# Where the tiles of a two-layer decoder trunk begin in SBUF: every dynamic tile at a multiple of 256 bytes, one weight form split in two halves

## The chip, the cores and the metric

One core of one Trainium2 chip runs the whole program. The metric is the device time of one execution in microseconds (us), the median of three runs. TensorE (PE) multiplies; VectorE (DVE), ScalarE (ACT) and GpSimd (POOL) prepare its operands and collect its results; SyncE (SP) issues the loads from HBM, and GpSimd issues some transfers too. SBUF is the memory from which TensorE reads, PSUM the one to which it writes. A place in SBUF is given here as a byte offset inside a partition; all 128 partitions hold the same layout.

## The reference

A sequence of 512 tokens of width 1024 goes through two layers. Each layer is a half-step SwiGLU, a mixer, and another half-step SwiGLU:

```
for l in range(2):
    x = x + 0.5 * swiglu(rms_norm(x, ffn_norm[l, 0]), w_gate[l, 0], w_up[l, 0], w_down[l, 0])
    h = rms_norm(x, mix_norm[l])
    m = hybrid_mixer(h, ...) if l == 0 else sparse_attention(h, ...)
    x = x + m
    x = x + 0.5 * swiglu(rms_norm(x, ffn_norm[l, 1]), w_gate[l, 1], w_up[l, 1], w_down[l, 1])

def swiglu(h, w_gate, w_up, w_down):
    return (silu(h @ w_gate) * (h @ w_up)) @ w_down
```

The SwiGLU's inner width is 2816. The hybrid mixer of layer 0 projects 1024 to 5656 columns, runs a Mamba-2 scan and an mLSTM on them, and projects 2048 columns back to 1024. The mixer of layer 1 is attention over 128 keys that an indexer picks for each query. All of it is in float32.

## The kernel before, in words

**Products.** A float32 weight block is cut by `made` and `both` into two float32r parts, a high and a low one: ScalarE copies the high part (line 361), VectorE subtracts to get the low part (line 363). Where `summed` is set, ScalarE writes the negated copy (line 391), a transfer from GpSimd's queue adds the block to it (line 392), and ScalarE writes the high part (line 393). The two parts together are called a form. The activations are cut the same way. `mm3` (lines 241 to 243) then multiplies with three matmuls: high by high, high by low, low by high. Each matmul has its own weight load, so TensorE alternates weight loads (128 columns) and matmuls.

**Seven instead of eight.** `seven` and `product_seven` compute a 2x2 block product with seven block products, from sums of the blocks. `unit_seven` is one unit of 256 of the 2816 inner columns, for gate and up together: seven block products, each with two halves of 128 columns (`s` = 0, 1), four row blocks (`q`) and three matmuls of 256 columns, so 7 x 2 x 4 x 3 = 168 matmuls. A SwiGLU has eleven units in groups of 4, 4 and 3; its first two units are done plainly by `unit` with matmuls of 512 columns, and nine by `unit_seven`. After each group `down` runs the output projection of that group as two more products of the seven-product kind, with as many row blocks as the group has units. That makes 9 x 168 + 4 x 7 x 2 x 3 x (4 + 4 + 3) / 2 = 1512 + 924 = 2436 matmuls of 256 columns in each of the four SwiGLUs. The hybrid mixer's input projection has six more such products with the weights as stationary operand, and four with the two operands exchanged (`tok=True`).

**Slots of the forms.** `ring("any")` deals out slots in turn. Slots 0 to 3 are parts of one static tile, `form`; the last one, slot 4, is a dynamic tile made by `one_form`. The hybrid mixer uses slots 0 to 3 only. The order of the tensor work is that of the program within a stream; the planner (`Plan`) orders the other engines around it by its costs and due times, and neither knows of addresses.

**Places.** The static tiles lie in this order: `raw` from byte 1152, which is (10 x 1024 + 512 + 16) x 4 = 43,072 bytes long; `form` from byte 44,224, 4 x 8192 bytes long; `ft` from byte 76,992, 16,384 bytes long. So the slots 0 to 3 begin at byte 192 past a multiple of 256 (192 mod 256), and the space for dynamic tiles begins at byte 93,376, which is 192 mod 256 too. An allocator places the dynamic tiles (activation forms `xf` and `hid`, the plain activations `xgn`, `one_form` and all the scratch) in that space, by their lifetimes. Before the change most of them sit at 0 mod 256, some at 192 and some at 224, the last because `hv` is 257 numbers wide. `one_form` sits at 0 mod 256. The dynamic space is nearly full: it is packed up to byte 228,160 of 228,192.

Of the kernel before, what the change touches and what calls it, by code (L numbers as in the profile page):

```python
# [11 lines left out]
F32R = mybir.dt.float32r  # L12
# [4 lines left out]
P = 128  # L17
# [26 lines left out]
PERIODS = [(p, _pieces(p, 4)) for p in (2 * math.pi * 512, 2 * math.pi)]  # L44
NRAW, NFORM = 4, 5
H = T // 2
# [160 lines left out]


class LazyFeat(Feat):
    def __getitem__(self, k):  # L210
# [3 lines left out]
class Trunk:  # L214
# [17 lines left out]

    def one_form(self):


        return Later(lambda: self.part.tile([P, 2, 1024], F32R, name="form", tag="form"))

# [136 lines left out]

    def made(self, block, summed=False):

        i, raw = block
        _, n, w = raw.shape
        j, f = self.ring("any")
        slot = f  # L380
        f = Later(lambda: slot[:, :, 0 : n * w].rearrange("p i (n w) -> p i n w", w=w))
        self.both(lambda: f, [("f", j, 0)], [("f", j, 1)], raw, [("raw", i)], summed)
        return j, f
# [105 lines left out]
    def seven(self, raws, xf, late, kept, evac):  # L489
# [6 lines left out]
        nq = len(xf)  # L496
        i, two = "sum", self.box
        t2 = i, two[:, 0 : nq * 256].rearrange("p (n w) -> p n w", w=256)

        def mul(ps, block, form, start, summed=False, f=None, ss=(0, 1)):  # L500
            j, f = made = f or self.made(block, summed)
            ps, psk = ps
            for s in ss:
                col = slice(s * P, (s + 1) * P)
                for q in range(nq):
                    self.times(
                        ps, psk, s, (j, lambda q=q, col=col: (f[:, 0, q, col], f[:, 1, q, col])),
                        lambda q=q: xf[q][0](form), xf[q][1](form), start and q == 0, q == nq - 1, not start, H, 0.355,
                    )
            return made  # L510
# [251 lines left out]
    def product_seven(self, raws, xf, kept, evac, tok, summed, scale):  # L762
# [3 lines left out]
        c11, c12, c21, c22 = evac  # L766
        two = "sum", self.box

        def mul(ps, block, form, start, ss=(0, 1), f=None):
            j, f = made = f or self.made(block, form in summed)  # L770
            bank, psk = ps
            for s in ss:
                col = slice(s * P, (s + 1) * P)
                for q in range(4):
                    if tok:
                        l = lambda q=q, col=col: [x[:, col] for x in xf[q][0](form)]
                        r = lambda q=q: (f[:, 0, q], f[:, 1, q])
                    else:
                        l = lambda q=q, col=col: (f[:, 0, q, col], f[:, 1, q, col])
                        r = lambda q=q: xf[q][0](form)  # L780
                    self.t(0.355, lambda l=l, r=r, s=s, q=q: self.mm3(
                        bank()[:, s * H : (s + 1) * H], l(), r(), start and s == 0 and q == 0, q == 3, True,
                    ), [("f", j, 0), ("f", j, 1)] + xf[q][1](form), [psk])
            return made
# [119 lines left out]
    def hybrid(self, nxt):  # L904
# [42 lines left out]
        def rows(c0, tag, width, func=None):  # L947

            half = [self.spot(tag, (NB, 2, width), 2) for _ in range(2)]
            at = lambda b, h: half[h // 2][0]()[:, b, h % 2]  # L950
            key = lambda b, h: (*half[h // 2][1], b, h)
# [101 lines left out]
    def gated(self, xs, hid, free):  # L1053

        nc, par = self.nc, self.par
        for grp in range(2):
# [13 lines left out]
            ps, psk = self.bank("hc")  # L1070
            col, ck = self.spot("hcol", (2, NB), 2)
            ms, rc = (lambda i=i, col=col: col()[:, i] for i in range(2))
# [281 lines left out]
    def mlstm(self, q, k, vt, og, g, hid):  # L1354
# [4 lines left out]
        (vx, vk), (ox, ok) = vt, og  # L1359
        st, stk = self.spot("cst", (4, 257), 1)  # L1360
        x4 = lambda t: t().rearrange("p (a b) -> p a b", a=4)
# [32 lines left out]
        for c in range(NB):  # L1394
            e, ek, qs, qsk, kt = ahead
            if c < NB - 1:
                ahead = weights(c + 1)
            ev, evk = self.spot("gev", (4, 4), 2)
            den, ss, rd, r = (lambda i=i, ev=ev: ev()[:, i] for i in range(4))
            part = lambda i: (*evk, i)  # L1400
            for h in range(4):
                ps, psk = self.bank("hc")

                def go(ps=ps, h=h, c=c, e=e, qs=qs):
                    nc.tensor.matmul(ps()[:, 0:257], e()[:, h], vx(c, h), start=True, stop=(c == 0))
                    if c:
                        nc.tensor.matmul(ps()[:, 0:257], qs()[:, h], st()[:, h], start=False, stop=True)

# [6 lines left out]
            if c < NB - 1:  # L1415
                for h in range(4):
# [4 lines left out]
                    if c:  # L1421
                        self.v(300, lambda ps=ps, h=h, c=c: nc.vector.scalar_tensor_tensor(
                            st()[:, h], st()[:, h], aa()[:, c, h : h + 1], ps()[:, 0:257], op0=ALU.mult, op1=ALU.add), [psk, sk, aak], [sk])
                    else:
                        self.v(257, lambda ps=ps, h=h: nc.vector.tensor_copy(st()[:, h], ps()[:, 0:257]), [psk], [sk])
            v4 = lambda issue, rd_, wr: self.v(4, issue, rd_, wr)
# [113 lines left out]
    def attention(self, nxt):  # L1540
# [4 lines left out]
        xg, xgk, rcol = self.xg, self.xgk, self.rcol  # L1545
        plan.stream = "filler"


# [329 lines left out]
        out(1, range(4, KC), True)  # L1878
        plan.stream = plan.floor = None

    def topk(self, sc, sk, m8, n):
# [14 lines left out]
    def run(self, stages=STAGES):  # L1896
        tc = self.tc
        with ExitStack() as ctx:
# [15 lines left out]
            self.rrow, raw = raw[:, 0:T], raw[:, T + 16 :].rearrange("p (i n) -> p i n", n=1024)  # L1914
            form = self.res.tile([P, NFORM - 1, 2, 1024], F32R, name="form")
            self.places = self.res.tile([P, 2, 8, H], F32, name="ft")
# [51 lines left out]
```

## Time and profile before

| | |
|---|---|
| median of three runs | 1998.28 us (1989.86 to 2009.0) |
| the profiled execution | 1994.66 us |
| its span, first to last instruction | 1992.6 us |
| mean granted TensorE clock | 0.994 |
| TensorE busy | 1945.2 us, 14594 matmuls |
| VectorE busy | 1633.1 us |
| ScalarE busy | 1266.3 us |

How to read the lines that follow: a row of the timeline is "start us, duration us, engine, line, operation, output<-inputs, shape, count", with idle time before it in brackets and what ended it. Matmuls overlap in the pipeline, so the duration of one (0.28 us for 256 columns) says little; the distance from one start to the next is what a matmul costs, and the prediction works with that distance. A row of the windows gives, for a stretch of time, its length and for each engine the busy time and the count of instructions, then the granted clock (PEclk) and the DMA share. A row of the groups gives line, engine, operation, operands, shape, count, then busy us, mean ns, and idle time before.

### The profile page before, as it was taken

Reading aid. Unit: us, or ns where it says so; the run is one execution under the profiler, and the core shown is the slowest. Engines: PE = TensorE matmul, PEld = TensorE weight load, DVE = VectorE, ACT = ScalarE, POOL = GpSimd, SP = SyncE. Lnnn points to the kernel's source line nnn. Section 1 sums busy time; section 2 is a strip of 40 time slices with the busy share of each in tenths; the row PEclk is TensorE's granted clock in tenths of the full one; section 3 lists DMA queues with packets and bytes.
Section 4 is the critical chain, followed back from the end, with each engine's and each line's share of the span. In section 5 each row is a group of like instructions: output and inputs, shape, how many; then the busy total and the mean of one; then the engine's idle time right before and its main releaser. Section 6 shows DMA issues by size and latency. Waiting matters only on the chain.

```text
span 1992.6 us, 36277 instructions
## 1 busy us (share of the span) xinstructions
PE 1945.2 (98%) x14594; PEld 1802.2 (90%) x14594; DVE 1633.1 (82%) x2383; ACT 1266.3 (64%) x1906; POOL 321.7 (16%) x401
## 2 busy tenths in 40 slices
PE   8999999999998999999999999999999999999998
PEld 6999999799887888999998899999956587999998
DVE  6888888987889558988888998978778747989886
ACT  6666656567768545657566575756756844757564
POOL 1000001222234110010002010000423521101010
PEclk9999999999999999999999999999999999999999
DMA  8566666467768342666665366666744302666564
GB/s 222 138 157 154 171 157 161 130 164 186 206 174 236 94 135 64 168 155 172 153 155 141 105 154 166 172 156 154 191 106 96 75 14 72 159 160 166 152 172 114
DMA packets 226609, 292.87 MB, mean 147 GB/s; under 512 B 15037, under 2 KB 196489, under 8 KB 225929
## 3 DMA queue, kind: packets, MB, share of 16 engines
q1 hardware_dynamic: 200728, 199.30, 32.4%
q0 software_dynamic: 25632, 91.24, 24.4%
q8 instruction: 114, 1.87, 0.4%
q14 instruction: 55, 0.44, 0.1%
q10 hardware_dynamic: 80, 0.02, 0.0%
HBM read 192.96 MB, written 6.33 MB: 100 GB/s over the span
## 4 chain that ended last, share of the span: by engine, by line
PE 77%; DMA 8%; DVE 8%; issue 5%; ACT 1%; POOL 1%; SPq 0%; POOLq 0%; ACTq 0%; DVEq 0%
PE pA L242 9%; PE pA L243 9%; PE pA L241 9%; PE pD L241 4%; PE pD L242 4%; PE pD L243 4%; DMA form<-raw 3%; PE hm L241 3%; PE hm L242 3%; PE hm L243 3%; PE pB L241 2%; PE pB L242 2%; PE pB L243 2%; DVE form L363 2%; DMA raw<-in_hy_w_in 2%
## 5 line engine op out<-in xcount | busy, mean ns | idle before, releaser
L363 DVE TENSOR_TENSOR form<-raw,form 128x1024 fp32r<-128x1024 f32 (+2 forms) x382 | 455.9, 1198 | 98.8 <-ACT form L361 97.1
L361 ACT ACTIVATE form<-raw 128x1024 fp32r<-128x1024 f32 (+2 forms) x382 | 392.3, 1030 | 219.1 <-DVE raw L356 148.2
L392 POOL DMA_DIRECT2D form<-raw x172 | 150.2, 874 | 1322.7 <-ACT form L391 1271.4
L356 DVE TENSOR_TENSOR raw<-raw 128x1024 f32<-128x1024 f32 (+2 forms) x281 | 334.8, 1196 | 21.6 <-DMA raw<-in_ffn_w_down 11.6
L241 PE MATMUL pA<-xf,form 128*128 128x256 f32 x1152 | 321.8, 279 | 0.0
L243 PE MATMUL pA<-xf,form 128*128 128x256 f32 x1152 | 321.4, 279 | 0.0
L242 PE MATMUL pA<-xf,form 128*128 128x256 f32 x1152 | 321.2, 279 | 0.0
L391 ACT ACTIVATE form<-raw 128x1024 fp32r<-128x1024 f32 (+1 forms) x172 | 178.4, 1038 | 159.3 <-PE pD L243 73.6
L241 PEld LDWEIGHTS pA<-xf,form 128*128 128x128 f32 x1152 | 217.3, 189 | 0.4
L243 PEld LDWEIGHTS pA<-xf,form 128*128 128x128 f32 x1152 | 217.3, 189 | 0.1
L242 PEld LDWEIGHTS pA<-xf,form 128*128 128x128 f32 x1152 | 217.2, 189 | 0.2
L242 PE MATMUL pA<-hid,form 128*128 128x256 f32 x704 | 198.4, 282 | 2.8 <-DVE hid L363 2.7
L243 PE MATMUL pA<-hid,form 128*128 128x256 f32 x704 | 197.3, 280 | 3.4 <-DVE form L363 3.4
L241 PE MATMUL pA<-hid,form 128*128 128x256 f32 x704 | 198.3, 282 | 0.9 <-DVE ft L356 0.3
L393 ACT ACTIVATE form<-raw 128x1024 fp32r<-128x1024 f32 (+1 forms) x172 | 176.6, 1028 | 0.0
L241 PE MATMUL pD<-xf,form 128*128 128x256 f32 x576 | 160.5, 279 | 0.0
L243 PE MATMUL pD<-xf,form 128*128 128x256 f32 x576 | 160.5, 279 | 0.0
L242 PE MATMUL pD<-xf,form 128*128 128x256 f32 x576 | 160.4, 279 | 0.0
L356 DVE TENSOR_TENSOR ft<-ft 128x256 f32<-128x256 f32 (+2 forms) x296 | 151.5, 544 | 3.4
L242 PEld LDWEIGHTS pA<-hid,form 128*128 128x128 f32 x704 | 132.8, 189 | 4.7 <-DVE hid L363 4.6
L243 PEld LDWEIGHTS pA<-hid,form 128*128 128x128 f32 x704 | 132.8, 189 | 3.6 <-DVE form L363 3.6
L241 PEld LDWEIGHTS pA<-hid,form 128*128 128x128 f32 x704 | 132.7, 188 | 2.1 <-DVE ft L356 0.9
(452 smaller groups left out, 5342.2 us busy)
## 6 DMA issues: line engine op xcount, KB each, us to landing
form<-raw POOLq DMA_DIRECT2D x156, 512.0 KB, 5.6
raw<-in_ffn_w_gate SPq DMA_DIRECT2D x88, 512.0 KB, 4.0
raw<-in_ffn_w_up SPq DMA_DIRECT2D x88, 512.0 KB, 4.0
raw<-in_ffn_w_down SPq DMA_DIRECT2D x64, 512.0 KB, 4.2
raw<-in_hy_w_in SPq DMA_DIRECT2D x44, 512.0 KB, 4.4
raw<-in_ffn_w_down SPq DMA_DIRECT2D x32, 384.0 KB, 3.2
raw<-in_hy_w_out SPq DMA_DIRECT2D x16, 512.0 KB, 3.5
form<-raw POOLq DMA_DIRECT2D x16, 384.0 KB, 4.2
```

Source lines behind the costliest of these rows:

```text
L241: mm(out, l[0], r[0], start=start, stop=False)
L242: mm(out, l[0], r[1], start=False, stop=False)
L243: mm(out, l[1], r[0], start=False, stop=stop)
L356: (self.p if pool else self.v)(n, lambda: e.tensor_tensor(out(), x(), y(), op=op), reads, writes)
L361: self.s(n, lambda: nc.scalar.activation(hi(), src(), AF.Copy), srck, hik)
L363: n, lambda: nc.vector.tensor_tensor(lo(), src(), hi().bitcast(F32), op=ALU.subtract), srck + hik, lok
L391: self.s(n, lambda: nc.scalar.activation(f()[:, 1], raw, AF.Copy, scale=-1.0), rawk, lok)
L392: self.plan.add("gpsimd", 0.85, lambda: nc.gpsimd.dma_start(f()[:, 1], raw, accum_op=ALU.add), rawk + lok, lok, 5.5)
L393: self.s(n, lambda: nc.scalar.activation(f()[:, 0], raw, AF.Copy), rawk, hik)
```

## The change

Three things are done to the places of tiles; no instruction is added to or removed from TensorE's work.

1. Widths of scratch tiles are rounded up so that each tile is a multiple of 256 bytes, and the static `form` tile grows by 16 numbers. The static tiles then end at byte 93,440, which is 0 mod 256, and all dynamic tiles begin at 0 mod 256. The four static slots stay at 192.
2. `one_form` becomes a dynamic tile of 10,240 bytes whose form begins 192 bytes into it; in the attention mixer it is an 8192-byte tile with the form at its start.
3. In each seven-product with weights as stationary operand, the first form that falls on slot 3 and isn't `summed` is laid out in two halves of 4096 bytes for its two halves of columns, the second half 4160 bytes after the first (`parted`, `Halves`). By these sizes the first begins at 44,224 + 3 x 8192 = 68,800 (192 mod 256) and the second at 72,960 (0 mod 256). The change's own short description calls the half at 0 the first one; by the sizes it is the second. Either way one of the two halves of that form is at 0 mod 256 and the other at 192.

```diff
-NRAW, NFORM = 4, 5
+NRAW, NFORM, SPLIT = 4, 5, 3
...
+class Halves:
+    def __init__(self, ap):
+        self.ap = ap
+    def __getitem__(self, i):
+        _, part, q, col = i
+        return self.ap[:, part, q, col.start // P]
...
-    def one_form(self):
-        return Later(lambda: self.part.tile([P, 2, 1024], F32R, name="form", tag="form"))
+    def one_form(self, close=False):
+        size, at = (8 * H, 0) if close else (10 * H, 48)
+        make = lambda: self.part.tile([P, size], F32R, name="form", tag="form")
+        return Later(lambda: make()[:, at : at + 8 * H].rearrange("p (i w) -> p i w", i=2))
+
+    def parted(self, n):
+        x = self.split
+        return bass.AP(x.tensor, x.offset, [x.ap[0], [4 * P, 2], [P, n], [8 * P + 16, 2], [1, P]])
...
-    def made(self, block, summed=False):
+    def made(self, block, summed=False, part=False):
...
+        if j == SPLIT and part and not summed and not self.parts_done:
+            self.parts_done, f = True, Halves(self.parted(n))
+            self.both(lambda: f.ap, [("f", j, 0)], [("f", j, 1)], raw.rearrange("p n (s c) -> p n s c", s=2), [("raw", i)], False)
+            return j, f
...
-            half = [self.spot(tag, (NB, 2, width), 2) for _ in range(2)]
+            half = [self.spot(tag, (NB, 2, -(-width // 8) * 8), 2) for _ in range(2)]
...
-            col, ck = self.spot("hcol", (2, NB), 2)
+            col, ck = self.spot("hcol", (16, NB), 2)
...
-        st, stk = self.spot("cst", (4, 257), 1)
+        st, stk = self.spot("cst", (4, 272), 1)
...
-            ev, evk = self.spot("gev", (4, 4), 2)
+            ev, evk = self.spot("gev", (16, 4), 2)
...
+        self.rings["any"][1][-1] = self.one_form(True)
...
+        self.rings["any"][1][-1] = self.one_form()
...
-            form = self.res.tile([P, NFORM - 1, 2, 1024], F32R, name="form")
+            form = self.res.tile([P, (NFORM - 1) * 2048 + 16], F32R, name="form")
+            self.split = form[:, SPLIT * 2048 : SPLIT * 2048 + 2064]
+            form = form[:, 0 : (NFORM - 1) * 2048].rearrange("p (n i w) -> p n i w", i=2, w=1024)
```

More of the change, by code (lines that the diff above doesn't have):

```diff
@@ L496, in seven @@
         nq = len(xf)
-        i, two = "sum", self.box
+        i, two, self.parts_done = "sum", self.box, False
         t2 = i, two[:, 0 : nq * 256].rearrange("p (n w) -> p n w", w=256)
         def mul(ps, block, form, start, summed=False, f=None, ss=(0, 1)):
-            j, f = made = f or self.made(block, summed)
+            j, f = made = f or self.made(block, summed, True)
             ps, psk = ps
@@ L766, in product_seven @@
         c11, c12, c21, c22 = evac
-        two = "sum", self.box
+        two, self.parts_done = ("sum", self.box), False
         def mul(ps, block, form, start, ss=(0, 1), f=None):
-            j, f = made = f or self.made(block, form in summed)
+            j, f = made = f or self.made(block, form in summed, not tok)
             bank, psk = ps
@@ L947, in rows @@
         def rows(c0, tag, width, func=None):
-            half = [self.spot(tag, (NB, 2, width), 2) for _ in range(2)]
-            at = lambda b, h: half[h // 2][0]()[:, b, h % 2]
+            half = [self.spot(tag, (NB, 2, -(-width // 8) * 8), 2) for _ in range(2)]
+            at = lambda b, h: half[h // 2][0]()[:, b, h % 2, 0:width]
             key = lambda b, h: (*half[h // 2][1], b, h)
@@ L1406, in go @@
                     if c:
-                        nc.tensor.matmul(ps()[:, 0:257], qs()[:, h], st()[:, h], start=False, stop=True)
+                        nc.tensor.matmul(ps()[:, 0:257], qs()[:, h], st()[:, h, 0:257], start=False, stop=True)
                 self.t(0.9 if c else 0.45, go, [ek, vk(c, h), vk(c, h) + (1,)] + ([qsk, (*stk, h)] if c else []), [psk])
@@ L1422, in mlstm @@
                         self.v(300, lambda ps=ps, h=h, c=c: nc.vector.scalar_tensor_tensor(
-                            st()[:, h], st()[:, h], aa()[:, c, h : h + 1], ps()[:, 0:257], op0=ALU.mult, op1=ALU.add), [psk, sk, aak], [sk])
+                            st()[:, h, 0:257], st()[:, h, 0:257], aa()[:, c, h : h + 1], ps()[:, 0:257], op0=ALU.mult, op1=ALU.add), [psk, sk, aak], [sk])
                     else:
-                        self.v(257, lambda ps=ps, h=h: nc.vector.tensor_copy(st()[:, h], ps()[:, 0:257]), [psk], [sk])
+                        self.v(257, lambda ps=ps, h=h: nc.vector.tensor_copy(st()[:, h, 0:257], ps()[:, 0:257]), [psk], [sk])
             v4 = lambda issue, rd_, wr: self.v(4, issue, rd_, wr)
```

## The prediction

> **What bounds the kernel now.** The page comes first: busy times, then the chain of waits.
>
> ```profile
> span 1992.6 us, 36277 instructions
> ...
> PE 1945.2 (98%) x14594; PEld 1802.2 (90%) x14594; DVE 1633.1 (82%) x2383; ACT 1266.3 (64%) x1906; POOL 321.7 (16%) x401
> ...
> PE 77%; DMA 8%; DVE 8%; issue 5%; ACT 1%; POOL 1%; SPq 0%; POOLq 0%; ACTq 0%; DVEq 0%
> ```
>
> TensorE is busy for 98% of the span and carries 77% of the chain. So the question is what one matmul costs. The groups by shape say which matmuls the change touches: those of the seven-products with weights as stationary operand, of which each of lines 241, 242 and 243 issues the same number.
>
> ```profile
> L241 PE MATMUL pA<-xf,form 128*128 128x256 f32 x1152 | 321.8, 279 | 0.0
> ...
> L241 PE MATMUL pA<-hid,form 128*128 128x256 f32 x704 | 198.3, 282 | 0.9 <-DVE ft L356 0.3 <-ACT form L361 0.2 <-ACT hid L361 0.2
> ...
> L241 PE MATMUL pD<-xf,form 128*128 128x256 f32 x576 | 160.5, 279 | 0.0
> ...
> L241 PE MATMUL pD<-hid,form 128*128 128x256 f32 x352 | 98.4, 280 | 0.0
> ...
> L241 PE MATMUL hm<-xf,form 128*128 128x256 f32 x336 | 94.1, 280 | 0.0
> ...
> L241 PE MATMUL pB<-xf,form 128*128 128x256 f32 x288 | 80.0, 278 | 0.0
> ...
> L241 PE MATMUL pB<-hid,form 128*128 128x256 f32 x176 | 49.3, 280 | 0.0
> ```
>
> These are 3584 per line, on three lines, 10,752 matmuls. The windows of the four SwiGLUs' seven-products and of the hybrid projection show where they lie:
>
> ```profile
> core 0: us, PE busy (x) PEld busy (x) DVE busy (x) ACT busy (x) POOL busy (x), PEclk, DMA share, GB/s
> 61.20:348.80 287.60, 286.19 (x2444) 284.58 (x2443) 246.17 (x306) 185.66 (x246) 30.78 (x34) 1.00 0.64 161
> 791.70:1079.50 287.80, 286.87 (x2438) 286.01 (x2437) 249.54 (x308) 188.78 (x250) 31.07 (x34) 1.00 0.63 160
> 1128.50:1418.50 290.00, 285.87 (x2438) 284.80 (x2436) 254.42 (x313) 190.48 (x256) 29.66 (x32) 1.00 0.62 158
> 1697.30:1986.00 288.70, 287.40 (x2454) 286.40 (x2454) 246.83 (x305) 183.28 (x242) 24.94 (x29) 1.00 0.60 154
> 380.30:509.00 128.70, 121.47 (x1019) 120.07 (x1018) 110.49 (x147) 86.52 (x109) 27.09 (x27) 1.00 0.71 174
> ```
>
> The four SwiGLUs have 1 to 4 us without TensorE each, the projection 7.2. The mean is 286.19 / 2444 = 117.1 ns in the first, at a clock of 1.00. Is that a floor? The timeline of TensorE, read from start to start, says no. Its rows at the changes of product in the first SwiGLU:
>
> ```profile
> 50.24 0.39 PE L241 MATMUL pg<-xgn,form 128*128 128x512 f32 x1
> ...
> 52.96 0.39 PE L241 MATMUL pg<-xgn,form 128*128 128x512 f32 x1
> ...
> 61.20 0.28 PE L241 MATMUL pA<-xf,form 128*128 128x256 f32 x1
> ...
> 64.02 0.28 PE L241 MATMUL pD<-xf,form 128*128 128x256 f32 x1
> ...
> 66.89 0.28 PE L241 MATMUL pA<-xf,form 128*128 128x256 f32 x1
> ...
> 77.77 0.28 PE L241 MATMUL pA<-xf,form 128*128 128x256 f32 x1
> ...
> 80.65 0.28 PE L241 MATMUL pA<-xf,form 128*128 128x256 f32 x1
> ```
>
> From 61.20 to 64.02 a product of 24 matmuls runs, its form in a static slot (192) and its activations at 0: 2.82 / 24 = 117.5 ns. From 64.02 to 66.89 the form is the dynamic one, at 0 like the activations: 2.87 / 24 = 119.6. Then four products with forms at 192 again: (77.77 - 66.89) / 96 = 113.3. At 77.77 comes the dynamic form again, (80.65 - 77.77) / 24 = 120.0, and behind it 113.3 once more. So the same instruction in the same places has two speeds, and which holds depends on what came before. I call 113.3 fast, 117.8 slow, and the products with both operands at the same place even (119.6 to 120).
>
> The hybrid projection, whose forms are all in static slots, stays slow:
>
> ```profile
> 385.93 0.28 PE L243 MATMUL hm<-xf,form 128*128 128x256 f32 x1
> ...
> 435.99 0.28 PE L242 MATMUL hm<-xf,form 128*128 128x256 f32 x1
> 437.51 0.39 PE L243 MATMUL hm<-xf,form 128*128 128x256 f32 x1 [1.24 <-DMA form<-raw]
> ```
>
> 425 matmuls in 50.06 us, 117.8 ns each, and no fast stretch among them. And a fast stretch ends at a wait:
>
> ```profile
> 1302.16 0.28 PE L243 MATMUL pD<-hid,form 128*128 128x256 f32 x1
> 1302.77 0.38 PE L241 MATMUL pA<-hid,form 128*128 128x256 f32 x1 [0.33 <-DVE ft L356]
> 1302.99 0.28 PE L242 MATMUL pA<-hid,form 128*128 128x256 f32 x1
> ...
> 1305.70 0.28 PE L241 MATMUL pA<-hid,form 128*128 128x256 f32 x1
> ```
>
> Before 1302.16 the stream was fast; after the wait of 0.33 us it takes 2.71 / 23 = 117.8. Going so through the whole trace: with forms at 192 and activations at 0 the stream starts slow after the 512-column products, turns fast only behind an even product, and turns slow only at a start-to-start of 141 ns or more. Of 15 even products entered slow, 13 left it fast; all entered fast left it fast. One of the two that failed:
>
> ```profile
> 149.25 0.28 PE L241 MATMUL pB<-xf,form 128*128 128x256 f32 x1
> ...
> 152.14 0.28 PE L241 MATMUL pA<-xf,form 128*128 128x256 f32 x1
> ...
> 159.91 0.28 PE L241 MATMUL pA<-xf,form 128*128 128x256 f32 x1
> ```
>
> It took 2.89 / 24 = 120.4 and left 117.7 behind it (7.77 / 66). Where activations sit at 192 or 224 the distance is 116 to 120, with few fast stretches, and they spoil the state: behind even products at 192 the stream at (0, 192) is slow more often than not.
>
> **The change part by part.**
>
> *Classes of the 10,752.* By place and distance the trace has 3265 fast, 4419 slow, 2192 even, 804 with activations off 0 (117.3), and 71 across waits. Without the waits: 3265 x 113.3 + 4419 x 117.8 + 2192 x 119.6 + 804 x 117.3 = 370 + 521 + 262 + 94 = 1247 us.
>
> *Activations all at 0.* The 804 join the others, and nothing spoils the state any more.
>
> *The dynamic form at 192.* Some 1600 matmuls are even no longer. This takes away what makes the stream fast today.
>
> *The split form.* One half of a product, 12 matmuls (9 in the last group's `down`), is even, and the static form at 192 follows: a short even stretch in place of the long one. In the successful entries the distance reached a steady 120 within 8 matmuls, so 12 should do, though no row shows an even stretch that ends after 12. Following the ring of slots through the program, 52 such halves arise, 606 matmuls; four products in five get one, at the first, second, third, fifth or seventh step (three in four in the hybrid projection).
>
> *Sum.* I follow the state through the program with today's waits where they are: slow at the start of each SwiGLU and after each wait, fast with 13 chances in 15 behind a split form entered slow. That gives 7540 fast, 2535 slow, 606 even: 854 + 299 + 73 = 1226 us. The difference is 21 us. Were every entry to succeed it would be 22.5, with 7 in 10 it would be 18.
>
> *What takes from it.* 2.5 of the 21 are in the hybrid projection, where TensorE is idle for 7.2 of 128.7 us on forms and loads (the 1.24 us above is one): between none and all of it stays, I count half, as its chain is shared with the loads. Matmuls of 512 columns lose a little: even they take (52.96 - 50.24) / 12 = 226.7, at 192 (61.20 - 52.96) / 36 = 228.9, and a fifth of 768 changes over, 0.3 us. The attention's output projection, 8 x 16 x 3 = 384 matmuls by the code, keeps a mixture of places; at 4.5 ns for a quarter of them it is worth 0.4 us either way, and I leave it out. A quicker TensorE leaves VectorE less room; it runs at 247 of 288 us in a SwiGLU, but around the first units it is nearly full:
>
> ```profile
> 784.00:830.00 46.00, 46.00 (x359) 44.41 (x358) 41.72 (x53) 32.62 (x44) 4.45 (x5) 1.00 0.59 149
> 1121.00:1170.00 49.00, 48.80 (x384) 47.26 (x383) 45.10 (x57) 35.84 (x49) 4.42 (x5) 1.00 0.56 140
> 1690.00:1740.00 50.00, 49.63 (x395) 47.89 (x394) 46.15 (x61) 37.03 (x51) 5.21 (x6) 1.00 0.57 146
> ```
>
> 91 to 92%. Each further wait there costs itself, some 0.3 us, and some 50 slow matmuls, 0.2 us; I set 1 us aside. The copies into a split form write runs of 128 numbers instead of 1024, on ScalarE and VectorE; at 1.0 and 1.2 us each now they would have to be much slower to be seen. Nothing is moved past a queue.
>
> Together 21 - 1.2 - 0.3 - 1 = 18.5 us. Against the profiled execution's 1994.66 that is 1976. The median is 3.6 above it; as much of the spread of the runs may be this game of fast and slow, which the change makes less a matter of chance, I add only a quarter of that: **1977 us**.
>
> [...] The rows above have 113.3, 117.8 and 120.0 for one instruction at one clock. [...]
>
> **The rivals.**
>
> *Nothing.* What looks like an effect of places is one of something else that goes with the slots, the product's position for instance. For it: some 5-ns steps come without any instruction changed. Against it: 425 matmuls without an even product never turn fast, and every turn to fast stands behind one. Time: 1995. [...]
>
> *Too short a kick (slower than before).* Place: the even half of a split form. Twelve matmuls, entered in the middle of a form, may not bring the stream to the steady 120. Then nearly all is slow, as in the hybrid projection today: 10,075 x 117.8 + 606 x 119.6 = 1259 us, 12 more than 1247: 2007. It decides once fewer than about one entry in five succeeds. For it: the failure at 149.25; against it: 13 of 15.
>
> *Tile waits.* The dynamic space is full to 32 bytes and `one_form` grows by 2048. If a tile has to wait for an older one at each of the twelve starts of `down`, at 1.24 us as above or up to twice that, the waits take 15 to 30 us: 1991 to 2006. They decide above 18 us.
>
> *Half.* VectorE or the loads hold TensorE, and further waits throw it back to slow: half the gain, 1986.
>
> **How the numbers follow.** Forecast 0.62, half 0.16, nothing 0.07, too short a kick 0.08, tile waits 0.07. The forecast's own range is 1968 to 1985 (gains of 10 to 27, with the median's place unknown by 4). To hold 8 in 10 I go from 1966 to 1996, which takes in half and nothing. About 1% is what a measurement of this kernel can tell from no change, that is 1978 to 2018 against the median: three quarters of the forecast lie below it, 0.47; slower by over 1% needs tile waits beyond the bound above, or these and a short kick together, 0.05; the rest, 0.48, is within 1%.
>
> **What would show it.** In the changed kernel's timeline: a product with a split form has 12 matmuls at about 118 or 113 and 12 at 120, and the next starts at 113.3; the hybrid projection has fast stretches; no 256-column product of 24 even matmuls is left in the SwiGLUs; the four windows shrink from 288 to about 284 each. It is wrong if the products behind a split form stay at 117.8, if fast stretches end without a wait, or if TensorE's idle time in the windows grows by more than a few us.

## The result, and the profile after

The changed kernel takes 1980.21 us (median of 11 runs, 1971.74 to 1989.59). The kernel before, run on the same chip, takes 1991.46 us (median of 11 runs, 1987.68 to 2009.0). The ratio is 0.9933, with a 95% interval from 0.9906 to 0.9959: a small gain, 0.7%, and the interval excludes 1. The profiled execution went from 1994.66 to 1980.21 us, 14.45 us less; the medians of the eleven runs are 11.25 us apart. Forecast were 1977 us and 18.5 us less. The 1998.28 us known before the prediction was the median of the first three of the eleven runs of the kernel before.

The page of the changed kernel, the lines of the span, of the busy times and of the chain of waits:

```profile
span 1978.5 us, 36296 instructions
...
PE 1931.9 (98%) x14594; PEld 1787.8 (90%) x14594; DVE 1630.3 (82%) x2383; ACT 1265.2 (64%) x1906; POOL 320.0 (16%) x401
...
PE 77%; DVE 8%; DMA 8%; issue 5%; ACT 1%; POOL 0%; SPq 0%; ACTq 0%; POOLq 0%; DVEq 0%
```

TensorE is busy for 13.3 us less with the same 14594 matmuls; the busy time of no other engine moved by more than 3 us. The same five windows as before, the four SwiGLUs' seven-products and the hybrid projection:

```profile
core 0: us, PE busy (x) PEld busy (x) DVE busy (x) ACT busy (x) POOL busy (x), PEclk, DMA share, GB/s
62.40:347.30 284.90, 283.63 (x2442) 281.99 (x2441) 245.50 (x306) 185.54 (x246) 30.74 (x34) 1.00 0.64 162
789.90:1071.90 282.00, 281.27 (x2436) 280.19 (x2435) 247.97 (x307) 188.68 (x250) 31.00 (x34) 1.00 0.64 162
1121.30:1409.60 288.30, 283.71 (x2436) 282.65 (x2435) 254.93 (x314) 190.16 (x256) 29.60 (x32) 0.99 0.62 160
1685.60:1971.70 286.10, 283.92 (x2452) 282.85 (x2451) 246.02 (x305) 182.86 (x242) 24.89 (x29) 1.00 0.61 155
378.80:508.60 129.80, 121.83 (x1017) 120.18 (x1015) 110.80 (x146) 86.47 (x109) 26.14 (x27) 0.99 0.70 171
```

The SwiGLUs lose 2.7, 5.8, 1.7 and 2.6 us; about 4 each was forecast. The hybrid projection got 1.1 us longer.

Two split forms show why. In the timeline of TensorE (start, duration, line, operands), this is one in the first SwiGLU that did what was forecast. Its first half begins at 120.19, the half at 0 at 121.60, the next product at 123.03 and the one after that at 125.75:

```profile
120.19 0.28 PE L260 MATMUL pA<-hid,form 128*128 128x256 f32 x1
...
121.60 0.28 PE L260 MATMUL pA<-hid,form 128*128 128x256 f32 x1
...
123.03 0.28 PE L260 MATMUL pA<-hid,form 128*128 128x256 f32 x1
...
125.75 0.28 PE L260 MATMUL pD<-hid,form 128*128 128x256 f32 x1
```

12 matmuls at 117.5 ns, 12 at 119.2, then 24 at (125.75 - 123.03) / 24 = 113.3. The same four places of another split form, 124 us later:

```profile
244.15 0.28 PE L260 MATMUL pA<-hid,form 128*128 128x256 f32 x1
...
245.56 0.28 PE L260 MATMUL pA<-hid,form 128*128 128x256 f32 x1
...
247.01 0.28 PE L260 MATMUL pB<-hid,form 128*128 128x256 f32 x1
...
249.83 0.28 PE L260 MATMUL pA<-hid,form 128*128 128x256 f32 x1
```

117.5, then 120.8, then (249.83 - 247.01) / 24 = 117.5 again: this even half changed nothing. Inside it the distances are 121 120 124 118 117, over and over, where the half that works settles at a steady 120.

Counted through the trace by start-to-start distance and by the places of the operands, the classes are 6171 fast, 3872 slow and 606 even, 1228.1 us without the waits. Before it was 1247.0; forecast were 7540, 2535 and 606, 1226. The two measured sums don't hold equally many matmuls: 10,680 before and 10,649 now, because some 30 more starts fall across waits. Per matmul it is 1247.0 / 10,680 = 116.76 ns before and 1228.1 / 10,649 = 115.33 now, and for 10,680 matmuls that is 15.3 us less, not 18.9. Of 24 even halves entered slow, 12 turned the stream fast and 12 failed; 11 of the 12 that failed have the pattern of five. All even halves entered fast left it fast.

### The profile page after: what moved, and what is told of

Its sections match the earlier page's. It is cut to its first block, busy times and chain, and to the rows that moved or that the text cites. A ratio compares the mean times of both kernels' runs of the same rounds, so it can differ in the third digit from the quotient of the medians.

```text
span 1978.5 us, 36296 instructions
## 1 busy us (share of the span) xinstructions
PE 1931.9 (98%) x14594; PEld 1787.8 (90%) x14594; DVE 1630.3 (82%) x2383; ACT 1265.2 (64%) x1906; POOL 320.0 (16%) x401
## 4 chain that ended last, share of the span: by engine, by line
PE 77%; DVE 8%; DMA 8%; issue 5%; ACT 1%; POOL 0%; SPq 0%; ACTq 0%; POOLq 0%; DVEq 0%
PE pA L261 9%; PE pA L262 9%; PE pA L260 9%; PE pD L262 4%; PE pD L261 4%; PE pD L260 4%; DMA form<-raw 3%; PE hm L260 3%; PE hm L261 3%; PE hm L262 3%; PE pB L262 2%; PE pB L261 2%; PE pB L260 2%; DMA raw<-in_hy_w_in 2%; DVE ft L375 2%
## 5 line engine op out<-in xcount | busy, mean ns | idle before, releaser
L375 DVE TENSOR_TENSOR raw<-raw 128x1024 f32<-128x1024 f32 (+2 forms) x281 | 333.1, 1190 | 26.2 <-DMA raw<-in_ffn_w_up 11.4
```

The costliest lines, as they stand in the source:

```text
L375: (self.p if pool else self.v)(n, lambda: e.tensor_tensor(out(), x(), y(), op=op), reads, writes)
```

## The experiments

Places are mod 256 here, and the place of the weights is counted from that of the activations, unless both are given.

**The distances alone.** A program of its own: one accumulator, high and low parts at the distances of the real forms, and nothing running but TensorE.

```python
for at in SWEEP:                                  # 0, 16, ... 496 bytes
    go([(at, k) for k in range(40)])              # 120 matmuls
for n in LENGTHS:                                 # 1, 2, 3, 4, 6, 8, three matmuls each
    for lead in LEADS:                            # 12 to 16
        go([(112, k) for k in range(lead)] + [(0, k) for k in range(n)] + [(112, k) for k in range(16)])
```

> This kernel leaves the whole decoder out: it holds one weight form and one activation form in SBUF and runs streams of 256-column matmuls (weight load and matmul in turn, in the order of mm3), with no other work beside them. First 32 streams of 120 matmuls, the form 0 to 496 bytes past the activations' place in steps of 16. Then streams with the form at 448 (which is 192 mod 256, as in the changed kernel), an even stretch at 0 of 3, 6, 9, 12, 18 or 24 matmuls inside them, entered after 36, 39, 42, 45 or 48 matmuls, and 48 matmuls at 448 behind it. If the place alone makes the speeds: about 117.8 ns from start to start at 192 and 448, 120 at 0 and 256, and 113.3 behind an even stretch that has settled at 120, which needs about 8 matmuls, in about half of the entries. If something else than the place does it (the rival 'nothing' of the prediction): one speed at every place, and none changes behind an even stretch.

Its timeline of TensorE, the starts of two matmuls 48 apart, in the streams with weights at 64, 192 and 256:

```profile
74.94 0.28 PE L18 MATMUL acc<-mov,wts 128*128 128x256 f32 x1
...
80.38 0.28 PE L18 MATMUL acc<-mov,wts 128*128 128x256 f32 x1
...
194.98 0.28 PE L18 MATMUL acc<-mov,wts 128*128 128x256 f32 x1
...
200.64 0.28 PE L18 MATMUL acc<-mov,wts 128*128 128x256 f32 x1
...
254.77 0.28 PE L18 MATMUL acc<-mov,wts 128*128 128x256 f32 x1
...
260.53 0.28 PE L18 MATMUL acc<-mov,wts 128*128 128x256 f32 x1
```

113.3, 117.9 and 120.0 ns: the same three numbers as in the kernel, with every other engine idle. These streams all begin some 0.8 us behind the one before and differ in the place alone, and the numbers repeat after 256 bytes (at 320 it is 113.3 again, at 448 117.8). The other places lie between 116.7 and 120.0. One of the later 30 streams at 448 stood at 113.4 before its even stretch, so a start behind such a wait doesn't always mean slow. An even stretch of 3 matmuls turned none of four slow streams, one of 6 turned two of five, and stretches of 9 and more turned all that were tried. So 12 matmuls are enough, and the pattern of five was not seen in this program. New is the place 64: fast within five matmuls, with no even stretch ahead.

**The order and the length of the even part.** Three kernels, each with one edit to the changed one. In the first the half at 0 is multiplied first:

```diff
-            for s in ss:
+            for s in (1, 0) if isinstance(f, Halves) else ss:
...
```

The hybrid projection gets the same order at its own loop.

> As the changed kernel, but of a split form the half at 0 mod 256 is multiplied first, so that the even stretch begins where the product begins, and the half at 192 follows inside the same form. In the changed kernel 12 of 25 even stretches entered slow left the stream fast, against 13 of 15 before the change, where they began with the product and were 24 long. Theory A, the place of the entry decides (at a product's start the last slow distance is 115 ns, inside a form 117): 8 or 9 of 10 slow entries succeed, about 7500 fast matmuls in place of 6171, some 6 us less than the changed kernel, 0.990 of before. Theory B, the length decides (12 are too few): about half succeed as before, no change against the changed kernel, 0.9935 of before.

In the second the whole split form is at 0, so that 24 matmuls are even:

```diff
-        return bass.AP(x.tensor, x.offset, [x.ap[0], [4 * P, 2], [P, n], [8 * P + 16, 2], [1, P]])
+        return bass.AP(x.tensor, x.offset + 16, [x.ap[0], [8 * P, 2], [2 * P, n], [P, 2], [1, P]])
```

> As the changed kernel, but the form that it splits lies as a whole at 0 mod 256: an even stretch of 24 matmuls (18 in the last down) that begins with the product. Theory A (place of the entry) and theory B (length) both want 8 or 9 of 10 slow entries to succeed here; with the 606 more even matmuls at 119.8 in place of 113.3 or 117.8 the gain against the changed kernel is about 3 us, 0.992 of before. If neither holds, and it was chance or the spoiled places of before that made 13 of 15, about half succeed and it is 3 us slower than the changed kernel.

In the third no form is split, and all weights are at 192:

```diff
-        if j == SPLIT and part and not summed and not self.parts_done:
+        if False and part:
```

> As the changed kernel, with all its places, but no form is split: every form of the seven-products lies at 192 mod 256 and there is no even stretch in the SwiGLUs and the hybrid projection. If an even stretch is the only way to the fast speed: no fast stretch at all, 10,680 matmuls at 117.8 ns make 1258 us against 1228 in the changed kernel, 30 us more, 1.008 of before. If the speeds come from something else (the prediction's rival 'nothing'): as the changed kernel, 0.9935 of before.

Measured, as ratios to the kernel before on the same chip: 0.9917 (0.9892 to 0.9943), 0.9928 (0.9902 to 0.9953) and 1.0046 (1.0027 to 1.0065). The first two can't be told from the changed kernel. Without any even matmul the kernel is slower than before; its windows of the first and third SwiGLU:

```profile
core 0: us, PE busy (x) PEld busy (x) DVE busy (x) ACT busy (x) POOL busy (x), PEclk, DMA share, GB/s
61.90:352.50 290.60, 289.38 (x2443) 287.86 (x2442) 245.91 (x305) 185.60 (x246) 30.73 (x34) 1.00 0.64 159
...
1126.20:1419.50 293.30, 289.50 (x2436) 288.64 (x2436) 255.56 (x314) 190.94 (x257) 29.61 (x32) 0.99 0.63 157
```

10,651 of its matmuls are slow and 11 fast, 1255.8 us without the waits, 117.78 ns each. Against the 115.33 of the changed kernel the even halves are worth 26.2 us of matmuls to it (for its 10,649), and moving everything to (0, 192) without them would have cost time. Slow entries that turned fast: 16 of 22 with the even half first, 16 of 21 with 24 even matmuls; against 12 of 24 these counts are too small to say that either order or length helps. Failed entries of the latter repeat the pattern of five through all 24: the length of the even part isn't what fails.

**What turns the stream, and all forms at 64.** A program of streams that copy the entries, first on idle engines, then with the others at work; and two kernels without a split form, with all slots at 64, once with activations at 64 and forms at 128, once at 0 and 64. In both the static tiles are shifted for it: in the first the small norm columns move behind `ft`, in the second the static tiles begin 128 bytes earlier, taken from what `dynamic_dma_scratch_size` sets aside. The edit of the second:

```diff
-        size, at = (8 * H, 0) if close else (10 * H, 48)
+        size, at = (8 * H, 0) if close else (10 * H, 16)
...
-        if j == SPLIT and part and not summed and not self.parts_done:
+        if False and part:
...
-            form = self.res.tile([P, (NFORM - 1) * 2048 + 16], F32R, name="form")
+            form = self.res.tile([P, (NFORM - 1) * 2048 + 48], F32R, name="form")
...
-    nc = bacc.Bacc("TRN2", target_bir_lowering=False, num_devices=1, dynamic_dma_scratch_size=1024)
+    nc = bacc.Bacc("TRN2", target_bir_lowering=False, num_devices=1, dynamic_dma_scratch_size=896)
```

> Leaves the whole decoder out; 42 streams of products on one accumulator, activations at 0 mod 256. First ten streams: 30 to 42 matmuls with weights at 192 (slow), or at 0 (even), then 60 with weights at 64. Theory 'a distance': weights 64 past the activations always settle at 113.3 within some 10 matmuls, behind slow and behind even alike, 10 of 10. Rival 'a state there too': behind slow matmuls of 117.8 the stream at 64 stays at 117.8 and is fast only behind even ones, 5 of 10. The other 32 streams copy what the changed kernel does: 48 to 93 slow matmuls with weights at 192, a split form of 12 at 192 and 12 at 0, then 48 at 192; in the first 16 the other engines are idle, in the last 16 VectorE, ScalarE and a load write and read SBUF meanwhile. Theory 'phase': whether the even half turns the stream fast depends on the matmul of the five-matmul pattern (118 117 118 118 117) at which it begins, so about half of the first 16 fail, with 121 120 124 118 117 in the even half. Rival 'traffic': the first 16 all turn fast, and failures are in the last 16 alone, about 8.

> No split form; every static slot and the dynamic form begin 64 bytes (mod 256) past the activations of the stationary products (activations at 64 mod 256, forms at 128). Theory 'a distance': 64 past the activations a product of 256 columns takes 113.3 ns from any start: 10,680 x 113.3 = 1210 us, 18 less than in the changed kernel, so some 1962 us, 0.984 to 0.987 of the kernel before. Rival 'a state there too': the products with operands exchanged, which have the distance 64 in the kernel before already, show both 113.3 and 117.8; then the time depends on how often a wait throws the stream to slow, with nothing in the program that turns it back: between 1965 and 2010, and if it behaves as the kernel without a split form did, 2000 (1.005). Rival 'place in the row': the distance counts only with activations at 0 mod 256, so that this kernel is slow and the next one fast.

> The same with activations at 0 mod 256 and forms at 64 mod 256 (the static tiles begin 128 bytes earlier). Theory 'a distance': the same 1962 us, 0.984 to 0.987. Rival 'a state there too': as the run before, 1965 to 2010. Rival 'place in the row': 1962 here and about 2000 in the run before.

The timeline of the streams, TensorE: in the second stream 24 matmuls at 192 lie between the first two rows and 47 at 64 between the last two; in the seventh the same at 0 and at 64:

```profile
25.25 0.28 PE L20 MATMUL acc<-mov,wts 128*128 128x256 f32 x1
...
28.07 0.28 PE L20 MATMUL acc<-mov,wts 128*128 128x256 f32 x1
...
29.45 0.28 PE L20 MATMUL acc<-mov,wts 128*128 128x256 f32 x1
...
34.77 0.28 PE L22 MATMUL acc<-mov,wts 128*128 128x256 f32 x1
...
89.25 0.28 PE L20 MATMUL acc<-mov,wts 128*128 128x256 f32 x1
...
92.12 0.28 PE L20 MATMUL acc<-mov,wts 128*128 128x256 f32 x1
...
93.54 0.28 PE L20 MATMUL acc<-mov,wts 128*128 128x256 f32 x1
...
99.07 0.28 PE L22 MATMUL acc<-mov,wts 128*128 128x256 f32 x1
```

Behind slow matmuls at 192 (117.5 ns) the place 64 is fast: (34.77 - 29.45) / 47 = 113.2. Behind even ones (119.6) it is slow: (99.07 - 93.54) / 47 = 117.7. Five streams of five each. Both of my theories for this part fell: 64 isn't always fast, and its state is not the one of 192 either. An even stretch, which makes 192 fast, makes 64 slow.

The 32 copies of the split form: every even half turned or kept the stream fast, on idle and on busy engines, and no pattern of five appeared, whatever the matmul at which it began. The matmul at which the even half begins doesn't explain the failures: both the theory and its rival had forecast about eight failures. Traffic is less well tested: 14 of the last 16 streams stood at 113.3 already when the even half came, and the two at 117.8 turned.

The two kernels: 0.995 (0.9928 to 0.9973) and 0.993 (0.9909 to 0.995), no better than the changed kernel and not to be told apart. In the second, 7433 matmuls are fast and 3237 slow, 1223.9 us without the waits. The first two SwiGLUs are nearly all fast; behind some waits the stream is slow, and as nothing in the program turns it back, it stays so, in the last SwiGLU for over 200 us.

**What turns it back.** A program that goes from even matmuls to 12 at each of sixteen places and on to 64, and the same from 192.

> Leaves the whole decoder out; 64 streams, activations at 0 mod 256. The runs so far suggest two phases of TensorE: in phase A weights at 192 take 117.8 and weights at 64 take 113.3, in phase B the other way round, and an even stretch turns A into B. First 16 streams: 24 even matmuls (into B), 12 with weights at 0, 16, ... 240, then 30 at 64; next 16: 30 at 192 (A), the same 12, then 30 at 64. Theory 'two phases': some place, 128 by symmetry, turns B into A, so that its stream of the first 16 ends at 113.3 and not at 117.8; the even place turns A into B in the second 16. Rival 'one way': no place but a wait turns B into A: all of the first 16 end at 117.8. Last 32 streams: 24 at 192, a wait of varied length on VectorE, 24 at 192, 24 at 64, 12 even, 24 at 192. Theory: each wait leaves A (117.8, 113.3, then 113.3 behind the even stretch) or B (113.3, 117.8, 113.3), both among the 32. Rival 'a third phase', which would explain the even halves of the changed kernel that fail: some streams have 117.8 at 192 before and behind the even stretch, with 121 120 124 118 117 in it.

Of the streams that come from even matmuls, those with 0, 32, 48 or 64 in between end slow at 64; the other twelve end at 113.3. So 128 turns it, as the theory of two phases said, but so does 192, and most other places do. One way only it is not. Of the sixteen that come from 192 five end slow at 64, those with 0, 96, 160, 176 and 224 in between; the theory had named 0 alone. The waits of the last part didn't come about: VectorE had done its work before TensorE got there (a copy that it made at 412.89 us took 0.31 us, and ScalarE read the sum of the stream ahead only at 413.62). So the next program has the waits, and beside it a kernel that draws the consequence: as the kernel with (0, 64), but static slot 3 begins at 192.

```diff
-            form = form[:, 0 : (NFORM - 1) * 2048].rearrange("p (n i w) -> p n i w", i=2, w=1024)
+            slot = lambda i, at: form[:, i * 2048 + at : (i + 1) * 2048 + at].rearrange("p (i w) -> p i w", i=2)
...
-                raw=[0, [raw[:, i] for i in range(NRAW)]], any=[0, [form[:, i] for i in range(NFORM - 1)] + [self.one_form()]]
+                raw=[0, [raw[:, i] for i in range(NRAW)]], any=[0, [slot(0, 0), slot(1, 0), slot(2, 0), slot(3, 32), self.one_form()]]
```

> Leaves the whole decoder out; 66 streams, activations at 0 mod 256. First 16: 24 even matmuls, 24 with weights at 64 (slow there, as the run before showed), 12 at 0, 16, ... 240, then 24 at 64. Theory 'one product at 192 turns it back': the stream with 12 at 192 ends at 113.3; rival: once slow at 64 it stays slow whatever stands between. Two streams that go to and fro between 192 and 64, 24 each: theory, 113.3 throughout after the first change; rival, one of the two places is slow each time. Then 24 streams with a wait of varied length in the middle, 24 at 192, 24 at 64, 12 even, 24 at 192: theory, some of the waits leave a third phase, slow at 192 before and behind the even stretch, with 121 120 124 118 117 in it; rival, every even stretch turns 192 to 113.3 as in the 59 streams so far. The last 24: the wait with weights at 64 on both sides: theory, most waits leave 64 fast, some slow, as in the kernel with all forms at 64; 24 at 192 behind them turn all to 113.3 at 64.

> As the kernel with activations at 0 and forms at 64, but static slot 3 begins at 192: every fifth product of a SwiGLU, every fourth of the hybrid projection. Theory 'one product at 192 turns it back': a slow stretch at 64, which in that kernel lasted up to 120 us, ends at the next slot 3: some 8466 matmuls at 64, nearly all fast, and 2214 at 192, fast or slow: 10,680 x 113.3 = 1210 to 1220 us, 4 to 14 less than there (1224), so 1965 to 1975, 0.986 to 0.991. Rival: it turns nothing, and the products at 192 are slow when those at 64 are fast: 8466 x 114.7 + 2214 x 117 = 1230 us, 1985, 0.996.

The timeline of the program, TensorE: the first row is the first matmul at 64 in the stream that goes to and fro, the second its last, 119 matmuls and four changes of place later:

```profile
206.68 0.28 PE L19 MATMUL acc<-mov,wts 128*128 128x256 f32 x1
...
220.18 0.28 PE L21 MATMUL acc<-mov,wts 128*128 128x256 f32 x1
```

(220.18 - 206.68) / 119 = 113.4: once this stream is fast at one of the two places, it is fast at the other. Slow at 64 and then 12 matmuls at 192: those are still slow, and the next at 64 are fast. Most of the other places do that too; only 0, 32, 48 and 64 leave 64 slow. Of 23 waits at 192, 7 left the stream slow at 192 and at 64 as well, but behind the 12 even matmuls that followed all 24 streams stood at 113.3: the failing even half was not found here. 23 waits at 64 left it fast 21 times; and 24 matmuls at 192 made 64 fast in all of these 24 streams.

The kernel: 1972.92 us, 0.9905 (0.9879 to 0.9931). 9477 matmuls fast, 1160 slow, 1210.9 us without the waits. That is 113.84 ns each, against 115.33 in the changed kernel: 15.8 us for as many matmuls. The time fell by less.

**The failing even half, and places that change at every product.** The last program puts a wait of varied length, then 24 matmuls at 192 (or at 64), an even stretch of 12, and 24 at 192. The last kernel has slots 1 and 3 at 192 and slots 0 and 2 and the dynamic form at 64 (the end of one line, against the kernel above):

```diff
-[slot(0, 0), slot(1, 0), slot(2, 0), slot(3, 32), self.one_form()]
+[slot(0, 0), slot(2, 32), slot(1, 0), slot(3, 32), self.one_form()]
```

> Leaves the whole decoder out; 64 streams, activations at 0 mod 256: 24 matmuls with weights at 192 (first 32 streams) or at 64 (last 32), a wait of varied length on VectorE, 24 more with weights at the same place, 12 even, 24 at 192. In the run before 7 of 24 waits left the stream at 117.8 at 192 and at 64 alike. Theory 'third phase': it is this one in which the even half of the changed kernel fails; about 3 in 10 of the first 32 streams are slow behind the even stretch too, with 121 120 124 118 117 in it, and some of the last 32, all of them slow at 64 before the even stretch. Rival 'the rest of the kernel': what makes even halves fail is something these streams don't have (other engines' traffic, other accumulators): all 64 end at 113.3.

> As the kernel with slot 3 alone at 192, but slots 1 and 3 begin at 192 and slots 0 and 2 and the dynamic form at 64, so that the places change every product or two. Theory 'each change of place from 192 to 64 ends a slow stretch': the slow matmuls of 256 columns (1160 there) halve at least, which is worth 2.5 us, half of it given back in waits: 0.989 to 0.991 of the kernel before, 1970 to 1975 us. Rival: 192 is left slow more often, some 4390 matmuls at 192 at 116 to 117.8 instead of 114: 10 to 15 us more, 0.996.

Two neighbouring streams of the program, in the timeline of TensorE: for each the second matmul behind the wait, the first even one, the first at 192 behind them and the last one:

```profile
38.68 0.28 PE L20 MATMUL acc<-late,wts 128*128 128x256 f32 x1
...
41.39 0.28 PE L19 MATMUL acc<-late,wts 128*128 128x256 f32 x1
...
42.82 0.28 PE L19 MATMUL acc<-late,wts 128*128 128x256 f32 x1
...
45.42 0.28 PE L21 MATMUL acc<-late,wts 128*128 128x256 f32 x1
...
49.35 0.28 PE L20 MATMUL acc<-late,wts 128*128 128x256 f32 x1
...
52.05 0.28 PE L19 MATMUL acc<-late,wts 128*128 128x256 f32 x1
...
53.50 0.28 PE L19 MATMUL acc<-late,wts 128*128 128x256 f32 x1
...
56.21 0.28 PE L21 MATMUL acc<-late,wts 128*128 128x256 f32 x1
```

Both are slow behind the wait (117.8 and 117.4). The first has 12 even matmuls at 119.2 and then 23 at (45.42 - 42.82) / 23 = 113.0; the second 12 at 120.8, in the pattern of five, and then 23 at (56.21 - 53.50) / 23 = 117.8. The waits differ by 25 ns. Of 31 streams slow at 192 ahead of the even stretch 7 fail so, all with the pattern of five. They come at fixed lengths: start-to-start across the wait is 181, 261, 381, 460, 581, 661 and 781 ns, each 200 ns behind the last but one. So slow at 192 covers two states that look alike. The length of the wait doesn't choose alone: all seven streams were fast before the wait, three that were slow before waits of 180, 380 and 580 ns did not fail, and 859 ns, 198 behind 661, did not either. At 64 the waits of 217, 417, 617 and 816 ns leave it slow; but there the even stretch turned all four, which I had not expected.

The kernel that alternates: 1970.04 us (1965.58 to 1973.92), 0.9896 (0.9880 to 0.9913) of the kernel before. Its median is the lowest here, 2.9 us under that of slot 3 alone, whose interval (0.9879 to 0.9931) holds all of its own: the two can't be told apart. Its interval and the changed kernel's (0.9906 to 0.9959) overlap, and the two weren't timed side by side, so that it beats the changed kernel is likely but not shown. The time came out as forecast, the reason did not: sorted by the mean of five neighbouring distances, some 1040 of its matmuls are slow, and by the same sorting some 1190 with slot 3 alone, so they didn't halve. The longest slow stretch is 96 matmuls, against 144 with slot 3 alone and 1843 with all forms at 64. Its windows:

```profile
core 0: us, PE busy (x) PEld busy (x) DVE busy (x) ACT busy (x) POOL busy (x), PEclk, DMA share, GB/s
62.90:346.20 283.30, 280.49 (x2444) 278.35 (x2443) 245.13 (x305) 185.39 (x246) 30.80 (x34) 1.00 0.66 163
783.20:1064.00 280.80, 278.99 (x2437) 277.80 (x2436) 248.49 (x307) 188.49 (x250) 31.22 (x34) 1.00 0.65 163
1112.70:1397.90 285.20, 279.68 (x2436) 278.35 (x2435) 254.30 (x313) 190.33 (x256) 29.73 (x32) 1.00 0.65 161
1675.00:1957.00 282.00, 279.87 (x2452) 278.96 (x2451) 246.03 (x305) 182.63 (x242) 24.97 (x29) 1.00 0.63 158
379.30:504.70 125.40, 118.68 (x1016) 116.79 (x1015) 110.57 (x146) 86.41 (x109) 25.64 (x27) 1.00 0.72 177
```

The sums over the five windows of five kernels, one execution of each, with idle as length less TensorE's busy time:

| | length | TensorE busy | idle |
|---|---|---|---|
| no split form, all at 192 | 1291.2 | 1278.9 | 12.3 |
| before | 1282.8 | 1267.8 | 15.0 |
| changed | 1271.1 | 1254.4 | 16.7 |
| slot 3 alone at 192 | 1262.3 | 1240.9 | 21.4 |
| alternating | 1256.7 | 1237.7 | 19.0 |

By and large, the quicker TensorE is, the more it waits: of the 41.2 us of busy time saved from the first row to the last, 6.7 come back as idle time. The fourth row is out of step: it has more idle time than the quicker kernel below it. Who it waits for stands in the view of TensorE's waits (line, awaited engine and tile, us in total, times, longest), for the kernel before, the changed and the alternating one:

```profile
PE pA L242 <- DVE hid L363: 2.7, 8, 0.7
```

```profile
PE pA L261 <- DVE hid L382: 3.4, 9, 0.7
```

```profile
PE pA L261 <- DVE hid L382: 6.0, 12, 0.7
```

It is VectorE's subtraction that makes the low part of `hid`, the inner activations that `down` starts with: 8, 9 and 12 waits, each up to 0.7 us.

## Why the prediction was right or wrong

*The mechanism: right.* One instruction at three speeds by place (113.3, 117.8 and 120.0 ns), two of them (117.8 and 113.3) at the same place, and an even stretch that turns the one into the other: the program of streams (p1_places) shows it with nothing else running, and the kernel without even matmuls (e3_no_even, 117.78 ns each and 1.0046 of the kernel before) shows that the gain hangs on them.

*The classes: 15.3 us for a forecast 21.* The step that failed is "fast with 13 chances in 15 behind a split form entered slow", together with "today's waits where they are". It was 12 in 24; with 7 in 10, which the prediction had beside it, it would have been 18, and an estimate that goes on at that slope gives 14.4 at 12 in 24. The waits, too, grew by some 30 starts, and a wait can leave the stream slow: 7 of 23 at 192 did in p4_turns_back. One of the prediction's own signs of being wrong came half true: behind half of the split forms entered slow the stream stayed at 117.8. The reason for the step was wrong as well: I took the two failures in the trace before for rare accidents of an even stretch, and in the last program they are a state of their own, into which waits of certain lengths (181 to 781 ns from start to start) put a fast stream. That such a state fails without the rest of the kernel is shown there; that the 12 of 24 in place of 24 of 31 there is only a matter of the kernel's wait lengths is argued, not shown.

*Twelve matmuls are enough: right.* 9 are, and an even part of 24 fails as well. The rival "too short a kick" falls, though the even half does fail in half of its slow entries, well above the one in five below which the rival decided.

*"Nothing": fell.* It would need the places to be without effect. With nothing but the place changed and every other engine idle, p1_places has 113.3 ns at 64, 117.9 at 192 and 120.0 at 256: places do matter.

*"Half": not ruled out by the medians.* It wanted 9 us and further waits that throw the stream back to slow. The profiled executions differ by 14.45, the medians by 11.25, which is nearer to 9 than to 18.5; and the further waits came, as said above, with idle time up by 1.7 us in the five windows. But more was lost in the even halves that fail, which "half" did not have.

*"Tile waits": fell.* Idle time in the four SwiGLU windows is 1.3, 0.7, 4.6 and 2.2 us, against 1.4, 0.9, 4.1 and 1.3 before.

*The hybrid projection: half of its gain was counted, and none came in that profile.* It has its fast stretches, but idle time grew from 7.2 to 8.0 us, and behind a wait of 1.98 us for a transfer (`form<-raw`) the clock was granted at half for 3.4 us (0.50 from 481.1 to 484.3 us, where matmuls start 213 ns apart). The windows around that place:

```profile
core 0: us, PE busy (x) PEld busy (x) DVE busy (x) ACT busy (x) POOL busy (x), PEclk, DMA share, GB/s
470.00:480.50 10.50, 8.52 (x75) 8.33 (x74) 7.57 (x9) 8.81 (x13) 4.11 (x5) 1.00 0.83 183
480.50:485.00 4.50, 4.50 (x27) 4.24 (x27) 1.59 (x4) 1.06 (x1) 0.00 (x0) 0.62 0.54 157
```

In 4.50 us only 27 matmuls start, where 38 would at 117.8 ns: 1.3 us lost. The kernel before had such stretches too (0.50 from 1417.3 to 1418.5 us), but none in this window, where its granted clock is 1.00, and over the span it is the same 0.994. The third SwiGLU of the changed kernel ends at half clock too, behind a wait of 3.4 us (the granted clock is 0.72 from 1404 to 1410 us, 0.50 from 1406.6 to 1409.4); 2.9 us of matmuls at half clock fall into its window, against 1.3 before, from which I estimate 0.8 us more lost.

*What is late next: right in kind.* 1 us was set aside for VectorE and 1.2 for the projection, 2.2 in all; idle time in the five windows grew by 1.7, and the half clock took 1.3.

*The time.* 18.5 less than 1994.66 was forecast for the profiled execution, and 14.45 came. Of the 14.1 us by which its span fell, 11.7 lie in the five windows: 15.3 from the classes, less 1.7 of idle time and some 2 us at half clock. The other 2.4 lie outside the windows, for the most part in the mixers, where the sum had next to nothing, and what made them isn't shown. So the class gain was 5.7 short, and a gain that was not forecast made up for part of it: that is luck. The median of 1977 was 3.2 us low, within the range, and in part that is luck too: the kernel before came out 6.8 us quicker over eleven runs than over the first three, and by the medians the gain was 11.25 us, not 18.5. The gain of 0.7% lies in the case "within 1%", to which the prediction gave 0.48.

## What to carry to other kernels

When a stream of equal matmuls runs at two speeds, take start-to-start distances from the timeline, sort them by the SBUF places of both operands mod 256 bytes, and look at what came before; a mean over the stage hides it. Here weights at 64 or 192 past the activations are fast or slow by history, and with changes between the two places, in one slot of five or at every product or two, the slow stretches were at most 144 matmuls long, without any special layout: that is simpler than a stretch at equal places, and was at least as quick (0.9905 and 0.9896 of the kernel before, against 0.9933). When two sums of such distances are compared, see that they hold equally many matmuls. What a state's chance is should be measured in the state it is entered from; 13 of 15 in one mixture of waits was 12 of 24 in another.

## What the runs showed of the hardware

- With 128 x 128 weights loaded for each matmul of 256 float32r columns, the start-to-start distance depends on the weights' place less the activations', mod 256 bytes: in streams that start behind a wait of 0.8 us (p1_places) it settled at 113.3 ns at 64, 117.8 at 192, 120.0 at 0, and 116.7 to 120.0 at the other multiples of 16. At 64 and at 192 both 113.3 and 117.8 occur, by history (113.2 and 117.7 at 64 in p2_entries, 113.0 and 117.8 at 192 in p5_wait_then_even). The programs had the activations at 0 throughout; that the difference counts rests on the kernel with activations at 64 and forms at 128, which took 0.995 of the kernel before (e4_all_64), near the 0.993 of the one at 0 and 64 (e5_all_64_at_0).
- The state survives a change of place between 64 and 192 (113.4 ns through four changes, p4_turns_back), and which state stood behind a wait went with the wait's length and the state before it: the failures at 192 (up to 781 ns, but not at 859) and the slow streams at 64 came back every 200 ns, where waits were varied in steps of about 25 (p5_wait_then_even).
- Why the places act so is not settled by these runs.
